# Both attention layers project a normed x with unsplit float32 weights, and the routing stage moves to VectorE

## The chip, the cores and the metric

One core of one Trainium2 chip runs the whole program. The metric is the device time of one execution in microseconds (us); three runs of the kernel before gave 1461.74, 1466.64 and 1473.64 us, the median is 1466.64 us.

## The reference

The input is 256 tokens of width 1024, in float32. Two transformer layers come first: layer 0 with the even mixer, layer 1 with the odd mixer, each with its MLP. A second block follows: a mixer with a context, then a mixture of 16 experts of which each token uses two.

```python
h = modulate(rms_norm(x, norm_mix[layer]), sh1, sc1)
u = h @ w_in                      # even: 1024 x 2976, odd: 1024 x 3072
...
q, k = rms_norm(q), rms_norm(k)   # per head, then rope, softmax(q k) v
x = x + g1 * (o @ w_out)
x = x + g2 * squared_relu_mlp(modulate(rms_norm(x), sh2, sc2))
...
scores = sigmoid(t @ w_router)    # moe: 16 experts in 4 groups of 4
g_idx = argmax(sum of the best two of each group)
out = out + gate[:, e:e + 1] * ((silu(a) * b) @ w_down[e])
```

The vectors sh1, sc1, g1, sh2, sc2, g2 are the columns of `silu(c) @ ada_w + ada_b`.

## The kernel before, in words

Tokens lie in two tiles of 128 (t = 0, 1). A product that needs full precision is made of three matmuls: weight and activation are each held as a rounded part "hi" (float32r) and the rest "lo", and `mm3` (L333 to L335) adds hi·hi, hi·lo and lo·hi in PSUM. A weight tile of 128 x 1024 is loaded into a "raw" tile by a DMA of SP's queue (L308), ACT casts it to hi (L321), and DVE subtracts to get lo (L322); in the even layer every fourth subtraction goes to POOL (`SHARE`). A raw tile is free again when lo is made. There are 4 raw, 5 hi and 5 lo tiles, and SP issues all loads in one order, so that a load that waits for its tile holds up the loads behind it.

- The even layer (`even`, phase 0). `first_columns` makes the normed x in columns and the first 672 projection columns (latents and rope key), with the scale and shift columns of layer 0 computed on the way by L755 from 8 MB of `adaN`. Then come two projections of 384 columns for the dilated values, the small projections `uq` and `ukv`, and four projections of 384 columns for dilated queries and keys, woven with the 8 heads of the first attention. `fill` puts 24 products of `adaT` (L458 on DVE, 512 KB each, two "ada" tiles) between them. The dilated attention and `even_out` follow.
- The first MLP (`mlp(0)`), 8 chunks, split weights.
- The odd layer (`odd`, phase 2). `norm_T` (called in the MLP's last chunk) leaves the normed x three times: hi in H0, lo in H1 and whole in A4. Query, key and value projections of the first attention (512 columns each) use `proj_steps` with hi and lo; the three of the second attention use `native_steps` (L378): one float32 matmul where `mm3` has three, with weights as they were loaded, into raw, hi and lo tiles in turn. A projection's epilogue `qk` runs over ACT (copy, square), POOL (rope halves L602, L603; reciprocal root L496, L497), DVE (L604, L605, L584, L636), then transposes on PE.
- The MLP of layer 1, the second block's mixer, then the routing: `before_route`, the `out2` projection with the router's logits behind each quarter, `route` (a chain of small DVE operations on 128 x 32 values), and `moe`, which normalises x into h2 on ACT, POOL and DVE (L1764 to L1773), splits it (L1777 on ACT, L1778 on POOL) and lets `experts` gather rows by one-hot matmuls (L1864) before the first expert product.

What differs between the two paths can be read from these lines:

```python
def split(self, hi, lo, src, scale=None, engine=None):      # L318
    ...
        self.nc.scalar.copy(hi, src)
        end = (engine or self.nc.vector).tensor_tensor(lo, src, hi, ALU.subtract)
...
def native_steps(self, st, hf, evac):                        # L371
    ws = sum([self.raw_unit(st) for _ in range(2)], [])
    ...
                    self.nc.tensor.matmul(pss[t], hf[:, k, t * P:t * P + P], ws[k], start=k == 0, stop=k == 7)
```

Of the kernel before, what the change touches and what calls it, by code (L numbers as in the profile page):

```python
# [11 lines left out]
F32R = mybir.dt.float32r  # L12
I32 = mybir.dt.int32
AF = mybir.ActivationFunctionType
ALU = mybir.AluOpType
# [25 lines left out]
EARLY_CONV = 1  # L41
ROPE_POOL = 1
# [3 lines left out]
SHARE = 4  # L46
# [6 lines left out]
EXTRA = [(), ("A4",), (), (), (), ()]  # L53
# [192 lines left out]
class Block:  # L246
# [114 lines left out]
    def raw_unit(self, st):  # L361

        ap, kt, w = st.next()
        ws = []
        for k0 in range(0, kt, 2):
            self.nnative += 1
            t = self.load(ap[:, k0 * w:k0 * w + 2 * w], ("raw", "hi", "lo")[self.nnative % 3])
            ws += [t[:, :w], t[:, w:2 * w]]
        return ws

    def native_steps(self, st, hf, evac):  # L371

        ws = sum([self.raw_unit(st) for _ in range(2)], [])
        pss = [self.ps(tag="pj") for _ in range(2)]
        for k0 in (0, 4):
            for t in range(2):
# [3 lines left out]
                if k0:  # L380
                    self.late.append([0, evac(t, pss[t], 512)])
                    yield
# [130 lines left out]
    def norm_T(self, rows, gates):  # L513
# [3 lines left out]
        hl = self.slot("H1", [P, 8, S], F32R)  # L517
        hh = self.slot("H0", [P, 8, S], F32R)
        self.h = hh, hl
        if self.phase == 1:  # L520
            self.hf = self.slot("A4", [P, 8, S])
        xns = self.slot("A0", [P, 2, D])
        for t, x in enumerate(self.x):
# [11 lines left out]
            for g in range(2):  # L535
# [7 lines left out]
                ends.append([nc.scalar.copy(hh[:, o, v], pv), V.tensor_tensor(hl[:, o, v], pv, hh[:, o, v], ALU.subtract)])  # L543
                if self.phase == 1:
                    nc.scalar.copy(self.hf[:, o, v], pv)
# [137 lines left out]
    def setup(self):  # L683
# [3 lines left out]
        c = self.T([P, CONST_W - 768], "consts")  # L687
# [33 lines left out]
        latents = self.first_columns()  # L721
        next(latents)
        nc.sync.dma_start(self.cols, A["cols"])
        self.trig(pf, inv)
        next(latents)
        nc.sync.dma_start(c[:, 178:434], A["consts"][:, 178:434])
        nc.sync.dma_start(c[:, 434:], A["consts"][:, 1202:])
        self.gains = self.slot("A5", [P, NGAIN1])
        nc.sync.dma_start(self.gains, A["gains"][:, :NGAIN1].to_broadcast([P, NGAIN1]))
        self.va = self.slot("A4", [P, 2048])  # L730
        nc.sync.dma_start(self.va[:, 1024:1792], A["consts"][:, 434:1202])
        self.dmasks = self.va[:, 1024:1792].rearrange("p (m k) -> p m k", m=3)
        self.gains2 = self.T([P, NGAIN - NGAIN1], "gains2")
        nc.sync.dma_start(self.gains2, A["gains"][:, NGAIN1:].to_broadcast([P, NGAIN - NGAIN1]))
# [33 lines left out]
    def first_columns(self):  # L768
# [16 lines left out]
        self.h = hh, hl = self.slot("H0", [P, 8, S], F32R), self.slot("H1", [P, 8, S], F32R)  # L785
# [3 lines left out]
        us = [self.unit(self.st) for _ in range(4)]  # L789
# [3 lines left out]
        us.append(self.unit(self.st))  # L793
        rooms = [self.slot(s, [P, 2, D]) for s in ("A4", "A5")]
        tiles.append([[r[:, i]] for r in rooms for i in range(2)])
        for t in tiles[2]:
            self.pe_load(t, 256)
        for (w, (c0, _)), ts in zip(PE_COLS, tiles):
            sums = self.ps(tag="po")
            for s, t in enumerate(ts):  # L800
                self.pe_part(sums, s, t, w)
# [5 lines left out]
            for k in range(j.start, j.stop):  # L807
                nc.scalar.activation(hh[:, k], xnT[:, k], AF.Identity, bias=cb[:, k:k + 1], scale=ca[:, k:k + 1])  # L808
                h = self.w(S)
                V.tensor_scalar(h, xnT[:, k], ca[:, k:k + 1], cb[:, k:k + 1], op0=ALU.mult, op1=ALU.add)  # L810
                V.tensor_tensor(hl[:, k], h, hh[:, k], ALU.subtract)
                wh, wl = us[k][:2]
                for i, (a, b) in enumerate(((0, 384), (384, 672))):
                    for t in range(2):
                        v = slice(t * P, t * P + P)
                        self.mm3(acc[i][t][:, :b - a], (hh[:, k, v], hl[:, k, v]), (wh[0][:, a:b], wl[0][:, a:b]), k == 0, k == 7)
                if len(us) < 8:
                    us.append(self.unit(self.st))
# [1267 lines left out]
```

## Time and profile before

| what | value |
|---|---|
| median of three runs | 1466.64 us |
| the profiled execution: its own time, its span | 1466.12 us, 1464.3 us |
| PE busy in the span | 1367.8 us (93%) |
| DVE, ACT, POOL busy | 1130.6, 834.2, 181.5 us |
| moved by DMA | 333.56 MB, 228 GB/s in the mean |

The shares are averages over stages with different limits, so the profile is read by stage: which engine is full in it, and which wait ends last. PE's busy time counts a matmul from its start to its modelled end, so that matmuls overlap; the pace of PE is the distance between starts. Stages of the program lie in the span so: first columns 0 to 46 us, the rest of the even layer to 222, its MLP to 405, the odd layer to 560, its MLP to 760, the mixer to 1120, routing to 1148, experts to the end.

### The profile page before, as it was taken

The page shows a single profiled execution, that of the slowest core. Times are in us where ns is not written, and L with a number is a line of the kernel's source. Part 1 is how long each engine was busy: PE and PEld are TensorE (multiplying, and loading weights), DVE is VectorE, ACT ScalarE, POOL GpSimd, SP SyncE. Part 2 cuts the span into 40 slices and gives each one's busy share as a digit, 9 for nine tenths or more (in the row PEclk, how much of TensorE's full clock was granted, in tenths as well). Part 3 has the DMA queues.
Part 4 walks back from the last instruction along what each step waited for, and adds up shares of the span by engine and source line. Part 5 has one row for each costly group of instructions (what it writes and reads, how often), then busy time and mean ns, then how long its engine had stood idle before and what let it go on. Part 6 is the DMA issues. An engine that isn't in the chain of part 4 may idle for free.

```text
span 1464.3 us, 20654 instructions
## 1 busy us (share of the span) xinstructions
PE 1367.8 (93%) x7402; PEld 1118.6 (76%) x7402; DVE 1130.6 (77%) x1880; ACT 834.2 (57%) x1329; POOL 181.5 (12%) x201
## 2 busy tenths in 40 slices
PE   6878889999999899999999999999996899999996
PEld 4767669888874467888989897677785788888884
DVE  4789867778784557799775789997766898888886
ACT  4565555445552464545764455655544687777774
POOL 0268420000053101000023000000003000000001
PEclk9989899999999989999999999999998899999998
DMA  9756547899944324878634766535552699999994
GB/s 350 251 181 226 172 144 248 305 326 322 333 146 147 113 87 139 285 269 300 233 105 137 241 234 205 173 124 169 177 180 87 214 359 338 330 328 322 319 346 147
DMA packets 93838, 333.56 MB, mean 228 GB/s; under 512 B 10656, under 2 KB 11808, under 8 KB 93216
## 3 DMA queue, kind: packets, MB, share of 16 engines
q1 hardware_dynamic: 93728, 332.17, 65.8%
q8 instruction: 60, 0.98, 0.3%
q14 instruction: 50, 0.41, 0.1%
HBM read 331.08 MB, written 1.05 MB: 227 GB/s over the span
## 4 chain that ended last, share of the span: by engine, by line
PE 62%; DVE 13%; DMA 11%; ACT 4%; issue 4%; POOL 4%; SPq 0%; POOLq 0%; ACTq 0%; DVEq 0%
PE pj L333 6%; PE pj L334 6%; PE pj L335 6%; PE ps L333 5%; PE ps L335 5%; PE ps L334 5%; DMA raw<-in_w_dram 5%; DMA ada<-in_adaT_dram 5%; PE ps L408 4%; DVE lo L322 3%; DVE ada L458 3%; PE pj L378 2%; ACT hi L321 2%; PE po L333 2%; PE po L335 2%
## 5 line engine op out<-in xcount | busy, mean ns | idle before, releaser
L321 ACT CAST hi<-raw 128x1024 fp32r<-128x1024 f32 (+3 forms) x325 | 327.3, 1018 | 230.8 <-DMA raw<-in_w_dram 70.5
L322 DVE TENSOR_TENSOR lo<-raw,hi 128x1024 fp32r<-128x1024 f32 (+4 forms) x315 | 380.3, 1218 | 99.4 <-ACT hi L321 96.8
L458 DVE CUSTOM_DVE_ANT_0 ada<-ada,crow 128x1024 f32<-128x1024 f32 x128 | 161.3, 1270 | 33.0 <-DMA ada<-in_adaT_dram 32.8
L333 PE MATMUL pj<-hi,H 128*128 128x512 f32 (+2 forms) x360 | 137.0, 384 | 5.7 <-ACT H L808 1.8
L334 PE MATMUL pj<-lo,H 128*128 128x512 f32 (+2 forms) x360 | 135.6, 378 | 5.1 <-DVE lo L322 4.3
L335 PE MATMUL pj<-hi,H 128*128 128x512 f32 (+2 forms) x360 | 133.3, 374 | 0.4 <-DVE H L543 0.4
L1191 PE MATMUL ps<-H,lo 128*128 128x256 f32 x408 | 116.0, 284 | 2.7 <-DVE lo L322 2.7
L333 PE MATMUL pj<-hi,A 128*128 128x512 f32 (+1 forms) x293 | 115.6, 395 | 2.1 <-DVE w L954 2.1
L334 PE MATMUL pj<-lo,A 128*128 128x512 f32 (+1 forms) x293 | 115.4, 394 | 1.1 <-DVE lo L322 0.9
L1189 PE MATMUL ps<-H,hi 128*128 128x256 f32 x408 | 116.0, 284 | 0.1
L1190 PE MATMUL ps<-H,hi 128*128 128x256 f32 x408 | 115.4, 283 | 0.0
L335 PE MATMUL pj<-hi,A 128*128 128x512 f32 (+1 forms) x293 | 114.4, 390 | 0.0
L333 PEld LDWEIGHTS pj<-hi,H 128*128 128x128 f32 x360 | 68.4, 191 | 22.4 <-issue 5.9
L334 PEld LDWEIGHTS pj<-lo,H 128*128 128x128 f32 x360 | 69.0, 192 | 17.0 <-DVE lo L322 7.0
L1191 PEld LDWEIGHTS ps<-H,lo 128*128 128x128 f32 x408 | 78.2, 192 | 3.9 <-DVE lo L322 3.9
L1189 PEld LDWEIGHTS ps<-H,hi 128*128 128x128 f32 x408 | 78.2, 192 | 0.9 <-ACT hi L321 0.3
L1190 PEld LDWEIGHTS ps<-H,hi 128*128 128x128 f32 x408 | 78.2, 192 | 0.4
L335 PEld LDWEIGHTS pj<-hi,H 128*128 128x128 f32 x360 | 68.3, 190 | 11.4 <-issue 1.9
L333 PE MATMUL ps<-hi,A 128*128 128x512 f32 x180 | 71.2, 396 | 0.0
L335 PE MATMUL ps<-hi,A 128*128 128x512 f32 x180 | 70.3, 391 | 0.0
L334 PE MATMUL ps<-lo,A 128*128 128x512 f32 x180 | 70.3, 390 | 0.0
L333 PEld LDWEIGHTS pj<-hi,A 128*128 128x128 f32 x293 | 55.5, 190 | 16.0 <-issue 4.4
(548 smaller groups left out, 3257.1 us busy)
## 6 DMA issues: line engine op xcount, KB each, us to landing
ada<-in_adaT_dram SPq DMA_DIRECT2D x128, 512.0 KB, 4.8
raw<-in_w_dram SPq DMA_DIRECT2D x128, 512.0 KB, 5.5
raw<-in_gu_dram SPq DMA_DIRECT2D x78, 512.0 KB, 5.9
raw<-in_in_dram SPq DMA_DIRECT2D x60, 512.0 KB, 4.5
raw<-in_down_dram SPq DMA_DIRECT2D x37, 512.0 KB, 5.6
crow<-in_gu_dram SPq DMA_DIRECT2D x34, 512.0 KB, 6.0
raw<-in_even_in_dram SPq DMA_DIRECT2D x24, 384.0 KB, 3.8
crow<-in_down_dram SPq DMA_DIRECT2D x18, 512.0 KB, 5.5
```

The costliest lines, as they stand in the source:

```text
L321: self.nc.scalar.copy(hi, src)
L322: end = (engine or self.nc.vector).tensor_tensor(lo, src, hi, ALU.subtract)
L333: mm(ps, ah, bh, start=start, stop=False)
L334: mm(ps, ah, bl, start=False, stop=False)
L335: mm(ps, al, bh, start=False, stop=stop)
L378: self.nc.tensor.matmul(pss[t], hf[:, k, t * P:t * P + P], ws[k], start=k == 0, stop=k == 7)
L408: self.nc.tensor.transpose(out, in_, self.ident[:p, :p])
L458: nc.vector.tensor_tensor_reduce(out=o, in0=wt, in1=r, scale=1.0, scalar=0.0, op0=ALU.mult, op1=ALU.add, accum_out=m[:, j:j + 1])
L1189: mm(ps[:, n % 2], wh, hh[:, k], start=k == 0 and n % 2 == 0, stop=False)
L1190: mm(ps[:, n % 2], wh, hl[:, k], start=False, stop=False)
L1191: mm(ps[:, n % 2], wl, hh[:, k], start=False, stop=k == 7 and n % 2 == 1)
```

## The change

- All six 384-column projections of the even layer, its first 672 columns, and the first three projections of the odd layer go through native float32 matmuls, one where there were three. No weight of `even_in` and `odd_in` is split; their tiles are used as loaded, from raw, hi and lo tiles in a fixed turn (`NATIVE`).
- The normed x of both layers is held once (`hf` in H0); hi and lo of it go, as do the cast and subtraction for them. In the odd layer the two halves are copied out of PSUM by ACT and DVE in turn.
- No subtraction goes to POOL in the even layer (`SHARE` goes); `uq`, `ukv` and `even_out` stay split, with DVE.
- In `first_columns` the gains are loaded earlier, masks and other constants later (behind the first value projection).
- Routing: the logits are made by float32 matmuls with tokens in rows from one unsplit x (`logits`); h2 starts as x·ar per quarter behind the residual sum, and becomes h2·rs + br by one DVE operation per token tile; hl is made by DVE behind the first one-hot mask; the first four expert tiles are loaded and split before the second half of `out2`; the first gather does all hi parts, then all lo parts, with DVE copying the latter.

```diff
-SHARE = 4
+NATIVE = ("raw", "hi", "lo") * 4 + ("hi", "lo")
-EXTRA = [(), ("A4",), (), (), (), ()]
+EXTRA = [(), ("A4",), ("A4",), (), (), ()]
...
         for k0 in range(0, kt, 2):
+            k1 = min(kt, k0 + 2)
             self.nnative += 1
-            t = self.load(ap[:, k0 * w:k0 * w + 2 * w], ("raw", "hi", "lo")[self.nnative % 3])
+            t = self.load(ap[:, k0 * w:k1 * w], NATIVE[self.nnative % len(NATIVE)])
...
-                ends.append([nc.scalar.copy(hh[:, o, v], pv), V.tensor_tensor(hl[:, o, v], pv, hh[:, o, v], ALU.subtract)])
-                if self.phase == 1:
-                    nc.scalar.copy(self.hf[:, o, v], pv)
+                if native:
+                    (V.tensor_copy if g else nc.scalar.copy)(self.hf[:, o, v], pv)
+                else:
+                    ends.append([nc.scalar.copy(hh[:, o, v], pv), V.tensor_tensor(hl[:, o, v], pv, hh[:, o, v], ALU.subtract)])
...
-        us = [self.unit(self.st) for _ in range(4)]
+        ws = [self.raw_unit(self.st)[0] for _ in range(4)]
...
+        def products(k):
+            for i, (a, b) in enumerate(((0, 384), (384, 672))):
+                for t in range(2):
+                    nc.tensor.matmul(acc[i][t][:, :b - a], hf[:, k, t * P:t * P + P], ws[k][:, a:b], start=k == 0, stop=k == 7)
+        columns(0)
+        for k in (0, 1, 2):
+            products(k)
+        columns(1)
+        products(3)
+        products(4)
+        columns(2)
+        for k in (5, 6, 7):
+            products(k)
...
-            self.proj(st, D, acts, f)
+            for _ in self.native_steps(st, self.hf, f):
+                pass
+            if c == 0:
+                nc.sync.dma_start(self.consts[:, 178:434], A["consts"][:, 178:434])
...
-                    yield from self.proj_steps(st, D, acts, f)
+                    yield from self.native_steps(st, self.hf, f)
...
-        for g in (qk_(("diff_q_norm", "diff_k_norm"), q1, False), val(v1, False)):
+        for g in (qk_(("diff_q_norm", "diff_k_norm"), q1), val(v1)):
...
-                self.out_T(self.x[t][:, j * 512:j * 512 + 512], self.xT, j * 4, t)
-                self.square(t, j)
+                self.to_T(o, self.x[t][:, s], 4, self.copied)
+                with self.behind(self.last_copy):
+                    self.square(t, j)
+                V.tensor_tensor(self.h2[:, t, s], self.x[t][:, s], self.ar[:, s], ALU.mult)
+                self.logits(t, range(4 * j, 4 * j + 4))
+            if j == 0:
+                self.sg = Stream(A["gu"], units(D, COLS_1024) * 16)
+                self.units0 = [self.expert_unit(self.sg) for _ in range(2)]
...
-        self.first = nc.scalar.copy(lT[:2 * NE], self.lps[:2 * NE, :S])
-        yield
-        for i in range(2):
-            nc.tensor.matmul(ps[:, i * NE:(i + 1) * NE], lT[:2 * NE, i * P:i * P + P], self.halves[:2 * NE], start=True, stop=True)
+        ps = self.lps
...
-        nc.scalar.mul(h2[:, 0], self.x[0], rs[0])
-        G_.tensor_tensor(h2[:, 0], h2[:, 0], self.ar, ALU.mult)
+        V.scalar_tensor_tensor(h2[:, 0], h2[:, 0], rs[0], self.br, op0=ALU.mult, op1=ALU.add)
...
-            G_.tensor_tensor(h2[:, 0], h2[:, 0], self.br, ALU.add)
-            V.scalar_tensor_tensor(h2[:, 1], self.x[1], rs[1], self.ar, op0=ALU.mult, op1=ALU.mult)
-        G_.tensor_tensor(h2[:, 1], h2[:, 1], self.br, ALU.add)
+        V.scalar_tensor_tensor(h2[:, 1], h2[:, 1], rs[1], self.br, op0=ALU.mult, op1=ALU.add)
...
-                G_.tensor_tensor(hl[:, t], h2[:, t], hh[:, t], ALU.subtract)
+                self.anchor[1:] = [V.tensor_tensor(hl[:, :, s], h2[:, :, s], hh[:, :, s], ALU.subtract)]
...
+            order = [(k2, q) for k2 in range(4) for q in range(2)] if g else [(k2, q) for q in range(2) for k2 in range(4)]
...
+                (V.tensor_copy if q and not g else nc.scalar.copy)(X[g][q][:, k2 * 2:k2 * 2 + 2], ps)
```

The scheduler sets each engine's order from this code. On PE at the start of the odd layer, where A is the normed x before its transposes (consts is the identity), H its transposed form and pj the projection's sum, the kernel before has:

```order
L408 MATMUL ps_3927<-consts_67,A_782_3902 128x128 x4
L333 MATMUL pj_4005<-hi_3983,H_780_3900 128x512
L334 MATMUL pj_4005<-lo_3984,H_780_3900 128x512
L335 MATMUL pj_4005<-hi_3983,H_779_3899 128x512
L333 MATMUL pj_4005<-hi_3983,H_780_3900 128x512
L334 MATMUL pj_4005<-lo_3984,H_780_3900 128x512
L335 MATMUL pj_4005<-hi_3983,H_779_3899 128x512
```

and the changed kernel has at the same place:

```order
L410 MATMUL ps_3515<-consts_67,A_708_3492 128x128 x4
L380 MATMUL pj_3571<-lo_3563,H_707_3491 128x512 x2
L380 MATMUL pj_3571<-raw_3565,H_707_3491 128x512
L410 MATMUL ps_3529<-consts_67,A_708_3492 128x128 x4
L410 MATMUL ps_3535<-consts_67,A_708_3492 128x128 x4
L380 MATMUL pj_3571<-raw_3565,H_707_3491 128x512
L380 MATMUL pj_3572<-lo_3563,H_707_3491 128x512 x2
```

Two rows of the weights take two matmuls in place of six, and the transposes of the second token tile stand behind three matmuls instead of behind twenty-two.

On DVE at the end of `out2`, where x, pj and w are residual, projection and product, A is h2 and es the routing's small tile, the kernel before has:

```order
L881 TENSOR_TENSOR w_10450<-pj_10389,row_10193 128x512
L882 TENSOR_TENSOR x_13_82<-x_13_82,w_10450 128x512
L504 SCALAR_TENSOR_TENSOR rs_10479<-ssx_79,rs_10479 128x1
L322 TENSOR_TENSOR H_2002_10256<-ps_10453,H_2001_10255 128x4x128
L1772 SCALAR_TENSOR_TENSOR A_2047_10476<-x_13_82,rs_10479,crow_10208 128x1024
L1716 SCALAR_TENSOR_TENSOR es_10491<-ps_10488,rs_10470,row_10241 128x16
L1716 SCALAR_TENSOR_TENSOR es_10491<-ps_10488,rs_10479,row_10241 128x16
L1718 TENSOR_SCALAR es_10491<-es_10491 128x32
```

and the changed kernel:

```order
L892 TENSOR_TENSOR x_13_82<-x_13_82,w_9908 128x512
L1780 SCALAR_TENSOR_TENSOR A_1900_9688<-A_1900_9688,rs_9924,crow_9657 128x1024
L1669 TENSOR_TENSOR A_1900_9688<-x_13_82,crow_9644 128x512
L1731 SCALAR_TENSOR_TENSOR es_9935<-ps_9763,rs_9924,row_9672 128x16
L506 SCALAR_TENSOR_TENSOR rs_9930<-ssx_79,rs_9930 128x1
L1731 SCALAR_TENSOR_TENSOR es_9935<-ps_9763,rs_9930,row_9672 128x16
L1783 SCALAR_TENSOR_TENSOR A_1900_9688<-A_1900_9688,rs_9930,crow_9657 128x1024
L1734 TENSOR_SCALAR es_9935<-es_9935 128x32
```

The wide operation of the second token tile has moved from ahead of the logits' first use to behind it, beside ACT's exponential; one wide and one half-wide operation stand ahead of it now, while x's transposes and squares are made.

## Rows read from the trace of the kernel before

**Rows 1.** The page's first part: busy time and share of the span, by engine.

```profile
PE 1367.8 (93%) x7402; PEld 1118.6 (76%) x7402; DVE 1130.6 (77%) x1880; ACT 834.2 (57%) x1329; POOL 181.5 (12%) x201
```

**Rows 2.** Stretches: us, busy PE, PEld, DVE, ACT, POOL, granted clock, DMA share, GB/s.

```profile
0.00:46.00 46.00, 32.12 (x232) 25.17 (x232) 21.91 (x91) 21.10 (x40) 2.11 (x10) 0.96 0.87 327
46.00:70.00 24.00, 20.73 (x108) 18.76 (x108) 19.21 (x35) 12.17 (x29) 10.25 (x15) 0.93 0.70 238
70.00:95.00 25.00, 18.83 (x88) 14.40 (x87) 18.04 (x40) 14.77 (x34) 18.28 (x29) 0.92 0.58 204
95.00:165.00 70.00, 60.22 (x319) 52.63 (x318) 63.51 (x130) 40.05 (x90) 54.36 (x47) 0.91 0.67 218
165.00:205.00 40.00, 38.68 (x222) 28.40 (x221) 31.12 (x82) 24.88 (x48) 4.35 (x3) 0.91 0.52 184
...
222.00:405.00 183.00, 177.75 (x1102) 159.92 (x1101) 142.92 (x187) 91.16 (x116) 0.73 (x2) 0.99 0.88 308
405.00:448.00 43.00, 38.71 (x178) 30.00 (x177) 34.27 (x59) 22.33 (x36) 22.65 (x20) 1.00 0.56 174
448.00:560.00 112.00, 105.42 (x402) 62.53 (x401) 60.93 (x176) 52.42 (x127) 16.98 (x22) 0.92 0.31 105
```

**Rows 3.** The chain of waits, 396 to 520 us: runs of native matmuls (start, us).

```profile
450.38 9.65 PE pj L378 x22
...
489.47 10.50 PE pj L378 x24
```

**Rows 4.** Timeline of PE: the even layer's projections, triples of 384 columns.

```profile
45.96 0.30 PE L335 MATMUL po<-hi,H 128*128 128x288 f32 x1
...
59.03 0.33 PE L333 MATMUL pj<-hi,H 128*128 128x384 f32 x1
...
59.55 0.33 PE L333 MATMUL pj<-hi,H 128*128 128x384 f32 x1
...
70.03 0.51 PE L333 MATMUL pj<-hi,A 128*128 128x384 f32 x2
```

**Rows 5.** Timeline of PE: a triple of 512 columns in the odd layer.

```profile
409.28 0.39 PE L333 MATMUL pj<-hi,H 128*128 128x512 f32 x1
...
409.96 0.39 PE L333 MATMUL pj<-hi,H 128*128 128x512 f32 x1
```

**Rows 6.** The subtractions of L322 alone, by stretch: DVE, POOL busy.

```profile
95.00:165.00 70.00, 19.51 (x17) 12.21 (x6) 0.91 0.67 218
```

**Rows 7.** The chain of waits from the odd layer's norm to its first scores.

```profile
410.46 1.14 DVE lo L322
...
442.70 0.61 DVE w L604
...
448.28 0.41 PE ps L665 x2
```

**Rows 8.** Timeline of DVE in the routing stage.

```profile
1119.95 0.68 DVE L881 TENSOR_TENSOR w<-pj,row 128x512 f32<-128x512 f32 x1
...
1124.27 3.36 DVE L1772 SCALAR_TENSOR_TENSOR A<-x,rs,crow 128x1024 f32<-128x1024 f32 x1
...
1128.22 1.88 DVE L1718 TENSOR_SCALAR es<-es 128x32 f32<-128x32 f32 x1 [0.30 <-ACT es L1717]
...
1130.52 1.89 DVE L1722 TENSOR_TENSOR es<-es,gains 128x32 f32<-128x32 f32 x1
1132.44 2.25 DVE L1726 TENSOR_TENSOR es<-es 128x24 f32<-128x24 f32 x1
1134.62 0.17 DVE L1727 TENSOR_TENSOR es<-es 128x16 f32<-128x16 f32 x1
```

**Rows 9.** Timeline of PE: the first one-hot gather and the first expert product.

```profile
1142.10 1.19 PE L1864 MATMUL po<-sc,O 128*128 128x256 f32 x4 [1.82 <-DVE row L1958]
...
1147.50 0.40 PE L333 MATMUL ps<-A,A 128*128 128x512 f32 x1
```

**Rows 10.** PE's waits in the expert stage, 1147 to 1445 us.

```profile
PE po L333 <- ACT A L1865: 0.4, 1, 0.4
```

More of the change, by code (lines that the diff above doesn't have):

```diff
@@ L792, in first_columns, with columns @@
             self.pe_load(t, 256)
-        us.append(self.unit(self.st))
-        rooms = [self.slot(s, [P, 2, D]) for s in ("A4", "A5")]
-        tiles.append([[r[:, i]] for r in rooms for i in range(2)])
+        ws += [self.raw_unit(self.st)[0] for _ in range(2)]
+        room = self.slot("A4", [P, 2, D])
+        tiles.append([[self.T([P, D], "crow", 2)] for _ in range(2)] + [[room[:, i]] for i in range(2)])
         for t in tiles[2]:
             self.pe_load(t, 256)
-        for (w, (c0, _)), ts in zip(PE_COLS, tiles):
+        ws += [self.raw_unit(self.st)[0] for _ in range(2)]
+        def columns(i):
+            w, (c0, _) = PE_COLS[i]
             sums = self.ps(tag="po")
-            for s, t in enumerate(ts):
+            for s, t in enumerate(tiles[i]):
                 self.pe_part(sums, s, t, w)
@@ L976, in kv_evac @@
             return f
-        self.share = SHARE
         for a, b in ((16, 24), (24, 40)):
@@ L1777, in moe, with low @@
                 nc.scalar.copy(hh[:, t], h2[:, t])
-                G_.tensor_tensor(hl[:, t], h2[:, t], hh[:, t], ALU.subtract)
+        M, sc, tmp = next(route)
+        def low():
+            for j in range(2):
+                s = slice(j * 512, j * 512 + 512)
+                self.anchor[1:] = [V.tensor_tensor(hl[:, :, s], h2[:, :, s], hh[:, :, s], ALU.subtract)]
+        self.low = low
         ps = self.ps()
@@ L1855, in gather @@
                 self.anchor[1:] = [last]
+                if self.low:
+                    with self.behind(last):
+                        self.low()
+                    self.low = None
             yield
             X[g] = [self.slot(f"A{g % 2 * 2 + q}", [P, 8, S], F32R) for q in range(2)]
[L1858 to L1866 removed]
+            order = [(k2, q) for k2 in range(4) for q in range(2)] if g else [(k2, q) for q in range(2) for k2 in range(4)]
+            for k2, q in order:
+                a = (hh, hl)[q]
+                ps = self.ps((P, 2, S), ("po", "ps")[q if g else k2 % 2])
+                for kk in range(2):
+                    k = k2 * 2 + kk
+                    for t in range(2):
+                        nc.tensor.matmul(ps[:, kk], a[:, t, k * P:k * P + P], pm[:, t].rearrange("p i s -> p (i s)"), start=t == 0, stop=t == 1)
+                (V.tensor_copy if q and not g else nc.scalar.copy)(X[g][q][:, k2 * 2:k2 * 2 + 2], ps)
+                yield
             for i in range(2):
```

121 lines of the change are left out of this document (50 added, 71 removed).

## The prediction

> **What bounds the kernel now.** The first thing to read is the page's line of busy time [rows 1]: PE is busy 1367.8 of 1464.3 us, DVE 1130.6, so almost every us that PE loses or saves should show in the time. That is an average. The second view, the windows by stage [rows 2], tells where it holds. In the first MLP (222 to 405 us) PE is busy 177.75 of 183 us and in the expert stage PE waits once, for 0.4 us, after its first product [rows 10]: both are bound by PE, and the change leaves their products alone. The stages that the change touches are limited otherwise. From 0 to 46 us PE looks full, but the DMA engines are at a share of 0.87 and 327 GB/s, the highest of the table. From 70 to 95 us POOL has 18.28 of 25 us and PE only 18.83. From 95 to 165 us DVE is the fullest, 63.51 of 70 us (91%), with PE at 60.22 and POOL at 54.36. From 165 to 205 us PE has 38.68 of 40. The odd layer's start (405 to 448 us) has PE at 38.71 of 43 us with a chain through DVE and POOL at its head and tail [rows 7]. The third view, the timeline, is for the routing: from DVE's last product sum at 1119.95 us [rows 8] to the first gather at 1142.10 us and the first expert product at 1147.50 us [rows 9] a chain of DVE operations decides, and PE has next to nothing.
>
> **The price of a native product.** The trace has native products already, in the second half of the odd layer: runs of 22 and 24 took 9.65 and 10.50 us [rows 3], together 20.15 us for 46, so 0.438 us for one of 512 columns. The three split matmuls for the same product start 0.68 us apart (409.28 to 409.96) [rows 5]. For 384 columns the split triple takes 0.52 us (59.03 to 59.55) [rows 4]. A native product of 384 isn't in the trace: by the share of columns 0.438 x 0.75 = 0.328 us, at most the 0.438 of the wider one, at least the 0.227 us of one split matmul of 512 (0.68 / 3) by the same share, 0.17. I take 0.328, the scaled row. For 288 columns likewise 0.39 split and 0.246 native. So a product saves 0.242 us at 512 columns, 0.192 at 384, 0.144 at 288. With 8 rows of weights and two token tiles, 16 products make a projection. PE saves 16 x (0.192 + 0.144) = 5.4 us in the first columns, 2 x 16 x 0.192 = 6.1 in the dilated values, 4 x 16 x 0.192 = 12.3 in dilated queries and keys, 3 x 16 x 0.242 = 11.6 in the odd layer: 35.4 us in all. How much of it is time depends on the stage.
>
> The Trainium skill speaks against this price: "FP8 and Floating Point Precision", section "TensorE Precision Notes", has true float32 take four passes through the array. Four passes at a third of the split triple would be 0.91 us for 512 columns; the rows show 0.438, about two passes, and the measurement decides. What four passes would make of the time is the last rival below.
>
> **Front and values, 0 to 70 us.** The next stage's first product, of `uq`, starts at 70.03 us [rows 4]; first columns end at about 46. PE's 5.4 + 6.1 us go, and with them ten subtractions and casts of weight tiles. What is late next is the DMA. What SP must bring up to the last value tile is, by the sizes in the code, x 1.05 MB, `adaN` 8.4, first columns 2.75, values 3.15, three fills of `adaT` 1.57, and the gains and constants that stand ahead, 1.9: 18.8 MB. At the 327 GB/s of the first 46 us that is 57.5 us, and PE is some 1.5 us behind the last tile. So `uq` starts at about 59 us, 11 us earlier. The rate held for 46 us so far, not for 58; I take -10. Bounds: -11.5 (all of PE's saving) and -3 (18.8 MB at the mean of the first 70 us, (327 x 46 + 238 x 24) / 70 = 296 GB/s, is 63.5 us, and 3 us more for the tail).
>
> **70 to 95 us.** `uq` and `ukv` stay split; the limit is the epilogue chain over POOL, which keeps its work. 0, with -6 as the end to which the free share of POOL (25 - 18.28) could shrink the stage.
>
> **95 to 165 us.** The four projections have 16 weight tiles. In this stretch DVE made 17 subtractions in 19.51 us (1.15 us each) and POOL 6 in 12.21 [rows 6]. Twelve on DVE go (-13.8 us), and `even_out`'s two from POOL's share come to DVE (+2.4). DVE then has 63.5 - 11.4 = 52 us, PE 60.2 - 12.3 = 48, POOL at most 42. With DVE at the same 91% the stage takes 57 us instead of 70: -13. The DMA allows it: up to 165 us the stages moved 327 x 46 + 238 x 24 + 204 x 25 + 218 x 70 = 41.1 MB, and at the first MLP's 308 GB/s that is 133 us, while the stage would now end at 165 - 10 - 13 = 142. That leaves little room, so I take -12. Bounds: 0, where the loads pace it at the old rate, and -16, PE's new 48 us at 89%.
>
> **165 to 205 us.** PE-bound; two subtractions wait on DVE (31.12 of 40 us) instead of POOL. 0, at worst +2.
>
> **Odd layer.** The first three projections take 48 x 0.438 = 21.0 us instead of 32.6, so PE's 38.71 us become 27. At the head DVE no longer makes lo of the normed x and of the first weights (the step at 410.46 us is one, 1.14 us [rows 7]) ahead of the second tile's norm, and the second tile's transposes stand behind three matmuls instead of 22. PE's idle time is 43 - 38.71 = 4.3 us; I count 2 of it as gained. At the tail the last key epilogue (DVE at 442.70, POOL, transposes, scores at 448.28, so 5.6 us, and some 2 us ahead of it) runs beside the value projection, which shrinks to 16 x 0.438 = 7.0 us; about 0.6 us of wait is new. -11.6 - 2 + 0.6 = -13. Bounds: -8 (the epilogues queue on POOL, 22.65 us of work in what would be 30) and -16 (all idle time goes). From 448 us on the products were native already: 0.
>
> **Routing.** On DVE the wide operation L1772, 3.36 us, stands in the chain; three small ones (L1718, L1722, L1726) take 1.88, 1.89 and 2.25 us while POOL runs the wide operations on h2, and their like takes 0.17 (L1727) when it doesn't [rows 8]. POOL's operations go, so these should fall to about 0.18 each: -5.5 us. In L1772's place stands L1783, not in the trace: at least the 0.68 us of a 512-wide operation, at most 3.36; two half-widths are 1.4, and it runs beside ACT's exponential. So -2 there. The lo part of h2 (two subtractions of 1.2 us by [rows 6]) stands on DVE behind the first mask, beside the hi gathers; if these don't hide it, +2.4. Logits in rows spare a copy and two transposes; counted at nothing. -7.5, bounds -3 and -10.
>
> **Experts.** PE waits for nothing; four tiles are there earlier: 0.
>
> **Sum.** -10 - 12 - 13 - 7.5 = -42.5 us. The profiled execution took 1466.12 us (span 1464.3 us), within 0.6 us of the median 1466.64, so no correction is needed: 1466.1 - 42.5 = 1423.6, say 1424 us. A measurement of this kernel can tell about 1%, 14.7 us, from no change.
>
> **Rivals.** (1) The even layer stays paced by its loads. For it: first columns and values come to the DMA's limit, and every product now waits for a tile directly, without a cast between that gave slack. Against: rates of 308 and 327 were held elsewhere. At the mean rate of the first 95 us, 272 GB/s, 41.1 MB take 151 us, not 142 to 143: +8.5, about 1432; at 258, the rate between this and the old mean of 249, 159 us: 1440.
> (2) The freed engines give more than counted: 70 to 95 us shrinks by 6, 95 to 165 and the odd layer by 16 each: 6 + 4 + 3 more, 1411. For it: POOL and DVE hinder each other in [rows 8], and POOL loses 12.21 us of subtractions in the crowded stage. Against: the 70 to 95 us stage is a chain of latencies.
> (3) The 22 us won in the even layer are given back in the first MLP, because its weights, at a DMA share of 0.88, come no earlier: 1424 + 22 = 1446. For it: 308 GB/s. Against: PE at 177.75 of 183 us there, so the loads keep ahead, and loads run ahead through free tiles as before.
> (4) Slower: native products cost more than the three that they replace, in the even layer's and odd layer's weights. Break-even is 0.68 us for 512 columns. At four passes of 0.227, 0.91 us, the odd layer gains 48 x 0.23 = 11 us, the even projections 96 x 0.173 = 17, the first columns 16 x 0.30 = 5; with routing's -7.5 this is +25, 1491 us. For it there is only the rule of four passes, from the Trainium skill's "FP8 and Floating Point Precision". Against it are the 46 products of [rows 3], which took less than half of that.
>
> **Chances.** Forecast 0.62, with a range of its own of 1412 to 1436; rival 1 0.18, rival 2 0.10, rival 3 0.07, rival 4 0.03. Rival 3's upper half, with part of rival 1's, reaches 1452 us, the bound of 1%: 0.03 of no change. So faster 0.94, same 0.03, slower 0.03. The range goes from 1406, below rival 2, to 1446, rival 3: it leaves out rival 4, half of rival 3 and the far end of rival 2, with what lies outside by a sum of unknown ends.
>
> **What would show it.** L380 at starts 0.44 us apart for 512 columns and 0.33 for 384; `uq`'s first product near 60 us (63 or later: rival 1); the stage of dilated queries and keys about 57 us long, its waits on DVE and not on DMA; the odd layer's norm to first scores 13 us shorter; the gap from the last product sum to the first expert product near 20 us instead of 27.6, with the small operations that follow L1718, L1722 and L1726 in the new code below 0.3 us each. The first MLP should be 183 us long still; 190 or more speaks for rival 3. L380 above 0.6 us for 512 columns would make the forecast wrong altogether.

## The result and the profile after

The changed kernel takes 1478.35 us in the median of 17 runs (1466.59 to 1482.03), the kernel before 1468.97 us beside it; the ratio is 1.0064 with a 95% interval of 1.0044 to 1.0083. The forecast was 1424 us, with a range of 1406 to 1446: a gain of 42 us was expected and a loss of 9 us came. The profiled execution of the changed kernel took 1482.03 us, its span is 1480.2 us: it is the slowest of the 17, so the two profiles stand 16 us apart where the medians stand 9 apart.

The page's line of busy time, to be held against [rows 1]:

```profile
PE 1394.9 (94%) x7238; PEld 1091.1 (74%) x7238; DVE 1079.8 (73%) x1838; ACT 793.0 (54%) x1268; POOL 132.5 (9%) x186
```

DVE lost 51 us of work, ACT 41, POOL 49, as the diff promises. PE gained 27 us where the prediction had taken 35 away. The windows of the changed kernel by stage, cut at the same events as [rows 2] (columns: stretch, length, busy PE, PEld, DVE, ACT, POOL, granted clock as a share of TensorE's full clock, DMA share, GB/s):

```profile
0.00:54.00 54.00, 38.35 (x200) 21.96 (x200) 12.12 (x72) 14.14 (x29) 2.79 (x11) 0.91 0.86 327
54.00:76.90 22.90, 21.92 (x75) 12.99 (x75) 13.40 (x32) 6.15 (x19) 3.35 (x11) 1.00 0.53 189
76.90:98.00 21.10, 16.61 (x79) 13.51 (x78) 14.90 (x35) 10.68 (x28) 14.49 (x24) 0.92 0.79 287
98.00:174.00 76.00, 64.86 (x256) 40.23 (x255) 52.50 (x134) 31.74 (x82) 36.76 (x45) 0.93 0.57 192
174.00:213.00 39.00, 38.92 (x230) 28.70 (x228) 26.22 (x71) 25.80 (x49) 0.44 (x1) 1.00 0.42 135
225.00:415.00 190.00, 184.05 (x1132) 163.35 (x1132) 144.18 (x188) 92.46 (x118) 0.73 (x2) 0.99 0.85 300
415.00:462.60 47.60, 45.75 (x131) 21.56 (x129) 19.82 (x46) 9.80 (x20) 17.74 (x20) 1.00 0.58 196
462.60:580.00 117.40, 110.57 (x408) 65.34 (x407) 65.09 (x182) 54.05 (x133) 19.17 (x25) 0.90 0.27 85
```

The reader is to see two things. The stage of dilated queries and keys (98 to 174 us) has 52.5 us of DVE, just what was forecast, and is 76 us long instead of the forecast 57, with PE at 64.86 where 48 were expected. The odd layer's start (415 to 462.6 us) has DVE at 19.82 of 47.6 us and PE at 45.75, at a full clock, where 27 were expected. The relief of DVE came; PE took it.

Why PE is fuller is seen in its timeline. First the even layer, native products of 384 columns, then the odd layer, of 512 (columns: start, us, engine, line, operation, tiles, sizes, count):

```profile
65.55 1.45 PE L380 MATMUL pj<-hi,H 128*128 128x384 f32 x4
66.84 1.45 PE L380 MATMUL pj<-lo,H 128*128 128x384 f32 x4
...
424.73 1.88 PE L380 MATMUL pj<-raw,H 128*128 128x512 f32 x4
426.45 1.88 PE L380 MATMUL pj<-hi,H 128*128 128x512 f32 x4
```

Four records of 384 columns start 1.29 us after the last four, so 0.32 us each, and of 512 columns 1.72 us, 0.43 each. These are the prices of the forecast (0.328 and 0.438). But a group of four records reads one weight tile for one half of the tokens, and a tile holds two rows of weights: that is two products, not four. All records of line L380 in the changed kernel, by the tile of the weights (count, shortest, median and longest in ns, first and last start in us, sizes):

```profile
L380 PE MATMUL pj<-hi,H x136: 483/591/1061, 56.1 to 509.5; 128*128 128x384 f32 x72, 128*128 128x512 f32 x64
L380 PE MATMUL pj<-lo,H x136: 483/592/1010, 61.7 to 517.1; 128*128 128x512 f32 x72, 128*128 128x384 f32 x64
L380 PE MATMUL pj<-raw,H x112: 483/540/1061, 54.6 to 518.9; 128*128 128x384 f32 x56, 128*128 128x512 f32 x56
```

That is 384 records. The program has 12 projections of 16 products, 192. The same count was there before the change, in the kernel before, for the three native projections that it had:

```profile
L378 PE MATMUL pj<-hi,A x32: 592/593/1061, 448.6 to 495.9; 128*128 128x512 f32 x32
L378 PE MATMUL pj<-lo,A x32: 592/593/1061, 451.3 to 503.6; 128*128 128x512 f32 x32
L378 PE MATMUL pj<-raw,A x32: 592/592/697, 456.4 to 505.3; 128*128 128x512 f32 x32
```

96 records for 48 products. The trace keeps two records for each native float32 product; [rows 3] counted records, and the prediction took them for products. So a product of 512 columns costs about 0.86 us, not 0.438, against 0.68 for the three split ones; of 384 columns 0.645 against 0.52.

The routing went as forecast. DVE's timeline from the last product sum on, which answers to [rows 8]:

```profile
1139.79 0.69 DVE L891 TENSOR_TENSOR w<-pj,row 128x512 f32<-128x512 f32 x1 [1.24 <-PE pj L335]
...
1145.48 1.27 DVE L1783 SCALAR_TENSOR_TENSOR A<-A,rs,crow 128x1024 f32<-128x1024 f32 x1
1146.68 0.17 DVE L1734 TENSOR_SCALAR es<-es 128x32 f32<-128x32 f32 x1
...
1147.27 0.19 DVE L1738 TENSOR_TENSOR es<-es,gains 128x32 f32<-128x32 f32 x1
1147.50 0.18 DVE L1742 TENSOR_TENSOR es<-es 128x24 f32<-128x24 f32 x1
```

and PE's, which answers to [rows 9]:

```profile
1155.08 1.20 PE L1885 MATMUL po<-sc,O 128*128 128x256 f32 x4 [1.82 <-DVE sc L1868]
...
1161.16 0.39 PE L333 MATMUL ps<-A,A 128*128 128x512 f32 x1
```

The three small operations fell from 1.88, 1.89 and 2.25 us to 0.17, 0.19 and 0.18, L1783 took 1.27 us where 1.4 was estimated, and the way from the last product sum to the first expert product is 21.4 us instead of 27.6.

### The profile page after: what moved, and what is told of

Its sections match the earlier page's. It is cut to its first block, busy times and chain, and to the rows that moved or that the text cites. A ratio compares the mean times of both kernels' runs of the same rounds, so it can differ in the third digit from the quotient of the medians.

```text
span 1480.2 us, 20182 instructions
## 1 busy us (share of the span) xinstructions
PE 1394.9 (94%) x7238; PEld 1091.1 (74%) x7238; DVE 1079.8 (73%) x1838; ACT 793.0 (54%) x1268; POOL 132.5 (9%) x186
## 5 line engine op out<-in xcount | busy, mean ns | idle before, releaser
L322 DVE TENSOR_TENSOR lo<-raw,hi 128x1024 fp32r<-128x1024 f32 (+2 forms) x279 | 337.1, 1218 | 106.4 <-ACT hi L321 104.5
L321 ACT CAST hi<-raw 128x1024 fp32r<-128x1024 f32 (+2 forms) x279 | 286.9, 1038 | 234.7 <-DMA raw<-in_w_dram 92.1
L460 DVE CUSTOM_DVE_ANT_0 ada<-ada,crow 128x1024 f32<-128x1024 f32 x128 | 156.2, 1228 | 42.2 <-DMA ada<-in_adaT_dram 42.0
L333 PE MATMUL pj<-hi,H 128*128 128x512 f32 (+1 forms) x192 | 76.1, 396 | 0.0
L334 PE MATMUL pj<-lo,H 128*128 128x512 f32 (+1 forms) x192 | 75.5, 393 | 0.0
L335 PE MATMUL pj<-hi,H 128*128 128x512 f32 (+1 forms) x192 | 74.3, 387 | 0.0
L333 PEld LDWEIGHTS pj<-hi,A 128*128 128x128 f32 x293 | 55.5, 190 | 18.2 <-issue 2.4
L322 DVE TENSOR_TENSOR lo<-crow,hi 128x1024 fp32r<-128x1024 f32 x52 | 62.5, 1222 | 7.2 <-ACT hi L321 6.7
L334 PEld LDWEIGHTS pj<-lo,A 128*128 128x128 f32 x293 | 55.5, 189 | 13.2 <-DVE lo L322 2.4
L335 PEld LDWEIGHTS pj<-hi,A 128*128 128x128 f32 x293 | 55.5, 189 | 10.8
```

What stands on the lines that cost most here:

```text
L333: mm(ps, ah, bh, start=start, stop=False)
L334: mm(ps, ah, bl, start=False, stop=False)
L335: mm(ps, al, bh, start=False, stop=stop)
L460: nc.vector.tensor_tensor_reduce(out=o, in0=wt, in1=r, scale=1.0, scalar=0.0, op0=ALU.mult, op1=ALU.add, accum_out=m[:, j:j + 1])
```

## The experiments

Two theories stood first: P, that a native product costs two records (0.86 us for 512 columns); and L, that it costs one and that loads take the gain. A third, S, came out of the first runs. Eleven kernels ran, each timed beside the kernel before. In the table a difference is that of the two medians (us) of the same comparison, the ratio has its 95% interval.

| run | median | difference | ratio |
|---|---|---|---|
| e1_route: new routing alone | 1461.28 | -9.4 | 0.994 (0.991 to 0.9971) |
| e2_odd: odd layer native alone | 1471.95 | +1.3 | 0.9986 (0.996 to 1.0011) |
| e3_even: even layer native alone | 1470.77 | +0.1 | 0.9997 (0.9973 to 1.0022) |
| e4_split: no native product in the odd layer | 1464.27 | -6.4 | 0.996 (0.9934 to 0.9987) |
| e5_half: changed kernel, narrow products | 1424.01 | -46.4 | 0.9706 (0.9662 to 0.9749) |
| e6_noroute: both layers native, old routing | 1480.99 | +10.6 | 1.0095 (1.0062 to 1.0128) |
| e7_route_split: e1 and e4 | 1457.38 | -13.1 | 0.9907 (0.9879 to 0.9935) |
| e8_twice: changed kernel, 48 products twice | 1517.47 | +47.0 | 1.0322 (1.0272 to 1.0371) |
| e9_rooms: changed kernel, other turn of tiles | 1471.06 | +0.8 | 1.0004 (0.9981 to 1.0026) |
| e10_before_rooms: before, other turn of tiles | 1464.34 | -6.0 | 0.9966 (0.994 to 0.9991) |
| e11_route_rooms: e1 and e10 | 1456.47 | -13.8 | 0.9884 (0.9855 to 0.9912) |

Where the profiles are compared below, the starts come from PE's timeline of each (us):

| start of | before | after | e5_half | e8_twice | e9_rooms | e10_before_rooms |
|---|---|---|---|---|---|---|
| first `uq` product | 70.03 | 76.86 | 65.67 | 76.27 | 74.55 | 70.97 |
| first scores, even layer | 98.61 | 102.41 | 92.18 | 102.99 | 100.56 | 99.58 |
| first dilated scores | 165.24 | 174.20 | 146.03 | 175.55 | 172.87 | 166.91 |
| first MLP, first product from a `hi` tile | 215.15 | 225.04 | 201.29 | 226.48 | 223.52 | 219.08 |
| odd layer's first product | 407.15 | 417.09 | 391.07 | 419.65 | 418.44 | 411.53 |
| odd layer's first scores | 448.21 | 462.63 | 423.06 | 506.39 | 463.99 | 452.58 |
| second MLP, first product of 256 columns | 577.20 | 594.29 | 534.17 | 636.82 | 585.72 | 575.11 |
| first gather | 1142.10 | 1155.08 | 1095.71 | 1197.79 | 1144.41 | 1138.77 |

In the text the two MLP rows are called the first and the second MLP for short. A single profile is good to a few us only: the first MLP starts at 215.15 us in the kernel before and at 219.08 in e10_before_rooms, with the same even layer.

**The parts alone.** e1_route is the kernel before with the new code from `out2` on:

```diff
-        nc.scalar.mul(h2[:, 0], self.x[0], rs[0])
-        G_.tensor_tensor(h2[:, 0], h2[:, 0], self.ar, ALU.mult)
+        V.scalar_tensor_tensor(h2[:, 0], h2[:, 0], rs[0], self.br, op0=ALU.mult, op1=ALU.add)
...
```

> The kernel before with the change of the routing stage alone. Both theories (the native products cost more than split ones; the native products are cheap and something else takes the gain back) leave this stage apart: the gap from the last product sum to the first expert product, 27.6 us before, should fall to about 21, and the time by 5 to 7.5 us. If it falls by less than 3 us, the routing is part of what went wrong.

It gained 9.4 us, more than the 5 to 7.5 expected here and inside the prediction's bounds of 3 to 10; in its profile the way from the last product sum to the first expert product is 20.2 us instead of 27.6. The routing isn't what went wrong.

e2_odd changes the first three projections of the odd layer, the norm's copies ahead of them, and the extra room A4:

```diff
-                yield from steps(f, native)
+                yield from self.native_steps(st, self.hf, f)
...
-EXTRA = [(), ("A4",), (), (), (), ()]
+EXTRA = [(), ("A4",), ("A4",), (), (), ()]
```

> The kernel before with the first three projections of the odd layer native, from one normed x; nothing else. Theory P (price): the trace keeps two records for each native product, so a product of 512 columns costs 2 x 0.43 = 0.86 us and not 0.438, against 0.68 for the split one; 48 products cost 48 x 0.18 = 8.6 us more, of which 2 to 4 come back at the stage's head: +4 to +7 us. Rival L (loads): the product is cheap, and waits for weight tiles take the gain: then PE shows waits for DMA in this stage, and without them the time would fall; -13 to 0 us.

The measured +1.3 us lies below theory P's range and just above L's; the interval by the ratio, -5.9 to +1.6, leaves P's range out. By the time alone, P missed. The stage itself speaks for P: from the odd layer's first product to its first scores the profile has 45.54 us, as in the changed kernel, where the kernel before has 41.06. Where the time came back is not shown.

e3_even changes the even layer alone:

```diff
-            self.proj(st, D, acts, f)
+            for _ in self.native_steps(st, self.hf, f):
+                pass
...
-                    yield from self.proj_steps(st, D, acts, f)
+                    yield from self.native_steps(st, self.hf, f)
```

> The kernel before with the even layer's change alone (native first columns, values, dilated queries and keys, order of the loads). Theory P: 96 products of 384 columns at 0.645 us instead of 0.52 cost 12 us, 16 rows of first columns some 3.6 us; what VectorE and GpSimd are relieved of gives back part of it where they were the bound (95 to 165 us): +4 to +12 us. Rival L: the products are cheap, PE waits for DMA in the front and the dilated stage; the time then lies between -22 and 0.

+0.1 us: below P's range again, and at the upper end of L's. The two layers alone cost nothing that can be measured, and together (e6_noroute, below) 10.6 us. That was the puzzle that led to theory S.

e4_split takes the native products out of the odd layer's second half instead:

```diff
-            yield from qk_(("moba_q_norm", "moba_k_norm"), q2, True)
-            yield from val(v2, True)
+            yield from qk_(("moba_q_norm", "moba_k_norm"), q2, False)
+            yield from val(v2, False)
```

> The kernel before with the odd layer's last three projections split as well, so that no native product is left in it. Theory P: 48 products go from 0.86 to 0.68 us on PE, -8.6 us if casts and subtractions keep up; -3 to -9 us. Rival L, with a native product at 0.438 us as the prediction had it: 48 x 0.24 = +11.6 us.

-6.4 us: theory L, by which it would have been 11.6 us slower, falls. It was taken for the price as well, too early, as e10_before_rooms shows.

**The price by itself.** e8_twice makes each native product of the odd layer's first three projections twice:

```diff
-                    self.nc.tensor.matmul(pss[t], hf[:, k, t * P:t * P + P], ws[k], start=k == 0, stop=k == 7)
+                    for i in range(self.twice):
+                        last = k == 7 and i == self.twice - 1
+                        self.nc.tensor.matmul(pss[t], hf[:, k, t * P:t * P + P], ws[k], start=k == 0 and i == 0, stop=last)
```

> The changed kernel with each native product of the odd layer's first three projections made twice (their sums are doubled), on a stretch where PE is full: the 48 more products are the price by itself. Theory P: 48 x 0.86 = +41 us, less what waits there now, so +36 to +42. Rival L, 0.438 us a product: +21 us or less.

The time rose from 1478.35 to 1517.47, 39 us for 48 products. The profile has it in the one stage: from the odd layer's first product to its first scores 86.74 us against 45.54, 41.2 us more, 0.858 us for a product. The page's line of busy time has 96 records more on PE for the 48 products (7334 against 7238), and PE's timeline shows eight records for four products, 3.43 us from start to start:

```profile
PE 1435.9 (94%) x7334; PEld 1108.8 (73%) x7334; DVE 1080.0 (71%) x1838; ACT 794.4 (52%) x1268; POOL 133.0 (9%) x186
```

```profile
425.57 3.60 PE L384 MATMUL pj<-raw,H 128*128 128x512 f32 x8
429.00 3.60 PE L384 MATMUL pj<-lo,H 128*128 128x512 f32 x8
```

This is theory P, shown.

**What the rest of the prediction was worth.** e5_half gives the products the price that the prediction had counted, by leaving out half of the columns in seven of eight:

```diff
-                    self.nc.tensor.matmul(pss[t], hf[:, k, t * P:t * P + P], ws[k], start=k == 0, stop=k == 7)
+                    n = w if k == 0 else w // 2
+                    self.nc.tensor.matmul(pss[t][:, :n], hf[:, k, t * P:t * P + P], ws[k][:, :n], start=k == 0, stop=k == 7)
```

> The changed kernel with seven of eight native products only half as wide (the right half of the columns of these products is left out of projections and first columns): with 0.86 us for a full product of 512 columns the mean is then 0.86 x (1 + 7 x 0.5) / 8 = 0.48 us, close to the 0.438 that the prediction counted. Theory P: with that price the rest of the prediction holds, some 35 to 45 us below the changed kernel in the first three projections of the odd layer and the even layer, and more where the odd layer's last three were native already: 1415 to 1445 us. Rival L (loads or chains take the gain): the loads are the same, the time stays within 10 us of the changed kernel.

1424.01 us, with products left out: loads and chains did not hold most of the gain back. That it meets the forecast to the digit is chance, since the sum is made otherwise. By the table of starts the odd layer begins 16.1 us earlier than in the kernel before (forecast for the even layer: 22), its first scores come 9.1 us sooner after that (forecast 13), and the way from there to the second MLP is 17.9 us shorter, in which the last three projections have their part: these were native before, and no forecast was made for them. The front is the exception: `uq` starts 4.4 us earlier than before, where 10 were forecast, so that at a low price too the front would have given less than half.

**Both layers, and neither.** e6_noroute is the whole change without its routing part; against the changed kernel:

```diff
-        V.scalar_tensor_tensor(h2[:, 0], h2[:, 0], rs[0], self.br, op0=ALU.mult, op1=ALU.add)
+        nc.scalar.mul(h2[:, 0], self.x[0], rs[0])
+        G_.tensor_tensor(h2[:, 0], h2[:, 0], self.ar, ALU.mult)
...
```

> The changed kernel with the routing stage of before: both attention layers native. The parts alone gave -9.4 us (routing), -2 (even +0, odd -2) against the kernel before, and all together +9.4. If the parts add up, as theory P has it with some 10 us more on PE, this is +10 to +18 us over before; if routing and layers hinder each other (a rival of its own: the early expert tiles or what follows on the loads), it is 0 to +3 us.

+10.6 us (by the ratio +9 to +19): the two layers together, inside theory P's range. It doesn't add up well with the rest, though: the changed kernel, which has the new routing besides, is at +9.4, so the medians give the routing 1 to 3 us here (by the differences or by 1480.99 - 1478.35) and 9.4 alone. In the profiles it shortens its stage here too, to 21.4 us from the 27.9 of e6_noroute. By the ratios it is worth 0.3%, give or take 0.4, which the 0.6% of e1_route doesn't contradict; whether layers and routing hinder each other stays open.

e7_route_split is e1_route with the edit of e4_split:

```diff
-            yield from val(v2, True)
+            yield from val(v2, False)
...
```

> The kernel before with the new routing stage and with the odd layer's last three projections split too: no native product at all. If the two add up (-9.4 and -6.4 us), 1453 to 1458 us, below both kernels. Rival L, with a native product cheaper than a split one, would have this above the run with the routing alone, 1461.

1457.38 us: the two gains add within 3 us, and this kernel is faster than both the kernel before and the changed one.

**The stall in the odd layer.** Together +10.6, alone +1.3 and +0.1: something in the single runs must have hidden the cost. For e3_even the profiles show what, a stall that the other kernels have on ACT, at the loads of the output projection. In the changed kernel, ACT's timeline:

```profile
486.07 1.03 ACT L321 CAST hi<-raw 128x1024 fp32r<-128x1024 f32 x1
492.89 1.04 ACT L321 CAST A<-raw 128x1024 fp32r<-128x1024 f32 x1 [5.78 <-DMA raw<-in_odd_out_dram]
...
494.79 0.49 ACT L650 COPY pt<-ps 128x384 f32<-128x384 f32 x1
```

and PE's beside it:

```profile
491.81 1.12 PE L380 MATMUL pj<-raw,H 128*128 128x512 f32 x2
495.34 1.65 PE L1289 MATMUL po<-A,pt 128*128 128x128 f32 x6 [2.41 <-ACT pt L650]
```

ACT stands for 5.78 us at a cast whose tile is not loaded; behind it in ACT's order are copies for which PE waits 2.41 us. SP's queue, from 440 to 540 us of the same profile and then of e9_rooms (below), tells why the tile is late:

```profile
SPq L308 <- PE pj L380: 34.5, 8, 13.9
```

```profile
SPq L308 <- PE pj L380: 27.7, 8, 6.9
```

Loads wait for tiles that native products still read (eight waits, 34.5 us in all, 13.9 the longest; in e9_rooms, which has no stall, the longest is 6.9). The kernel before has the same stall, PE waiting 4.12 us:

```profile
482.63 1.65 PE L1278 MATMUL po<-A,pt 128*128 128x128 f32 x6 [4.12 <-ACT pt L645]
```

Which rooms (the buffers of raw, hi and lo tiles) the last native weights use is set by a running count. In the kernels of before and after the last tile is a raw one. The native even layer alone moves the count, so that the last raw tile is the third from the end, and there is no such wait in that profile. In e2_odd the last tile is a hi one, and the one before it is raw; its wait is 2.02 us, so that the stall doesn't explain why e2_odd came out so cheap. e9_rooms, e10_before_rooms and e11_route_rooms have one line more, in the changed kernel, in the kernel before and in e1_route:

```diff
+        self.nnative += 2
         side = side()
```

> The changed kernel with the turn of weight tiles moved on by two ahead of the odd layer's last three projections, so that their last two tiles lie in hi and lo rooms and not the last one in a raw room. Theory S (stall): in the kernels of before and after, the first load of odd_out waits for a raw room that a native projection still holds, ScalarE's cast waits for the load, PE waits for copies queued behind the cast (4.1 us before, 2.4 us after, then a lower granted clock); the native even layer alone had moved this turn by chance, which hid its own cost. Without the stall -4 to -7 us against the changed kernel, 1471 to 1475. Rival: the turn does not matter, 1476 to 1480, and the even layer's cost comes from elsewhere.

> The kernel before with the same step of two in the turn. Theory S: the stall of 4.1 us and the lower clock behind it go, -4 to -7 us, about 1464, as much as splitting the last three projections gave (-6.4), which would mean that this gain came from the freed raw rooms rather than from the cheaper product. Rival: if the product's price made that gain, no change here, 1468 to 1472.

> The kernel before with the new routing and the step of two in the turn. Theory S: 1461.3 - 5 = 1455 to 1457 us, level with routing and all-split products (1457.4). Rival: 1461 us, as with the routing alone.

All three went as theory S has it: 1471.06 us against 1478.35 (-7.3), -6.0 us, and 1456.47 us. A window of 20 us from the same place, first of the changed kernel, then of e9_rooms (columns as above):

```profile
483.00:503.00 20.00, 17.59 (x51) 8.75 (x49) 12.71 (x35) 7.62 (x18) 6.10 (x7) 0.83 0.34 105
```

```profile
484.00:504.00 20.00, 20.00 (x63) 9.89 (x62) 15.71 (x48) 10.12 (x23) 7.33 (x9) 1.00 0.32 105
```

With the stall PE is idle for 2.4 us and its granted clock is 0.83 in the mean; without it 1.00. The two do not always go together, as e6_noroute shows, which has the changed kernel's turn and its wait:

```profile
493.39 0.94 PE L1289 MATMUL po<-A,pt 128*128 128x128 f32 x6 [2.42 <-ACT pt L650]
```

```profile
481.00:501.00 20.00, 17.58 (x57) 8.70 (x57) 12.98 (x35) 8.46 (x18) 7.46 (x8) 1.00 0.34 105
```

The profiles side by side, from the first odd scores to the second MLP:

| run | PE's wait behind the cast, us | length, us | granted clock |
|---|---|---|---|
| before | 4.12 | 128.99 | 0.93 |
| e1_route | 4.24 | 130.72 | 0.93 |
| e2_odd | 2.02 | 128.42 | 0.92 |
| after | 2.41 | 131.66 | 0.90 |
| e6_noroute | 2.42 | 124.35 | 0.96 |
| e3_even | none | 122.54 | 0.96 |
| e9_rooms | none | 121.73 | 0.96 |
| e10_before_rooms | none | 122.53 | 0.96 |
| e11_route_rooms | none | 127.16 | 0.91 |

The wait goes with the turn of the rooms in every run of the table. How much time follows it goes with the granted clock, which is low in e11_route_rooms without the wait and high in e6_noroute with it. So the 9.9 us between the changed kernel and e9_rooms in this table are not all the stall's, and its price is read from the medians: 7.3, 6.0 and, e11_route_rooms against e1_route, 4.8 us.

It follows also that freed raw tiles are enough for e4_split's gain (e10_before_rooms has -6.0 with the native products kept); that the cheaper product added anything there is not shown. Of the complete kernels e11_route_rooms and e7_route_split are the fastest; their intervals overlap.

## Why the prediction was wrong, point by point

**The failed step** is the price of a native product: "runs of 22 and 24 took 9.65 and 10.50 us [rows 3], together 20.15 us for 46, so 0.438 us for one of 512 columns". It was 0.438 us for one record, and a product has two. It measured 0.858 us (e8_twice). The step could have been caught in the trace of before: 96 records for three projections of 16 products each. Rival 4, to which 0.03 was given, is the mechanism that came: it set four passes of 0.227, 0.91 us. The Trainium skill had it so, in "FP8 and Floating Point Precision", section "TensorE Precision Notes" (true float32 takes four passes); the trace agrees, with 0.858 us, 3.8 times a third of the split triple. The prediction let its measurement decide against that page, and the measurement was misread. Rival 4's 1491 us were too many all the same: at the measured prices PE has 8.5 + 12.0 + 4.2 = 24.7 us more to do in both layers instead of 33, and not all of that became time, as the stages below show.

**The front** was forecast 10 us shorter with DMA as its bound. `uq` starts 6.83 us later. By the measured prices PE has 32 x 0.125 = 4.0 us more for the values, and a row of first columns takes about 2.35 us (the tile from 51.15 us on) against 2 x (0.52 + 0.39) = 1.82, so 4.2 for eight: 8.2 us. By place it is otherwise: the stage of first columns ends 8 us later (54 against 46) and the one of values is 1.1 us shorter (22.9 against 24.0). That loads bound the front is not borne out: in the first 54 us of the changed kernel PE's own waits for DMA come to 1.0 us. Nor was the price all that was wrong here, since e5_half had only 4.4 us of the 10; what held the rest was not followed.

**70 to 95 us**, counted at 0, became 3.0 us shorter from `uq` to first scores, inside the bounds given.

**95 to 165 us**, forecast -12: from first scores to dilated scores 71.79 us instead of 66.63, +5.2. DVE fell to 52.5 us as worked out. PE's 64 products of 384 columns cost 64 x 0.125 = 8.0 us more instead of 12.3 less, so PE is what is late; the relief gave back about 3.

**165 to 205 us and the first MLP** were counted at 0. From dilated scores to the first MLP's products it is 50.8 us instead of 49.9, and from there to the odd layer's first product 192.05, as before (192.00). Rival 3, a gain given back there, had no gain to take back here; e5_half, which had 13.9 us at the first MLP, kept them (189.8 us through it).

**The odd layer**, forecast -13: +4.5 us from its first product to its first scores. 48 x 0.178 = 8.5 us more on PE; 4 come back, of which 2.4 are idle time that the stage lost, about as forecast (PE idle 1.9 us of 47.6 instead of 4.3 of 43).

**Routing**, forecast -7.5: -6.2 us in the profiles of before and after, -9.4 in e1_route. Right in kind and size: the three small operations and L1783 in L1772's place come to -7.6. POOL's wide operations and the delays went together; no run moved POOL's alone.

**Experts**, counted at 0. They became some 2 us longer. The two windows, of the kernel before and then of the changed one, go from the first expert product to PE's last matmul (columns as above):

```profile
1147.50:1451.40 303.90, 303.06 (x1434) 251.12 (x1432) 265.48 (x270) 229.81 (x273) 0.00 (x0) 1.00 0.90 319
```

```profile
1161.16:1467.19 306.03, 305.04 (x1434) 251.00 (x1432) 266.71 (x273) 227.17 (x267) 0.00 (x0) 1.00 0.89 311
```

All six profiles with a native even layer have 306.0 to 307.1 us here and all seven with a split one 303.7 to 304.6, with the same 1434 records and a full clock. The routing is not the cause, as e3_even has it (306.85) and e1_route has not (303.72); why the same products run slower no run shows.

**The sum by the runs.** Routing gives -9.4 us (e1_route). Both layers cost 1471.06 - 1456.47 = 14.6 us, with the same routing and no stall in either (e9_rooms against e11_route_rooms). The stall costs 7.3 us after and 6.0 before, +1.3. Together +6.5, against the +9.4 measured. With the layers' cost from e6_noroute, 10.6 - 1.3 = 9.3 us, it would be +1.2. The medians are good to some 3 us each, so the layers' cost is known no better than 9 to 15 us. Of the 14.6 us the profiles place about 6.6 in the even layer (the first MLP starts at 224.6 us in the mean of five profiles with a native even layer, 218.0 in seven with a split one, which lie between 212.2 and 221.3), 3.9 in the odd layer's first half (45.5 against 41.6) and some 2 in the experts. The other 2 us lie within what single profiles differ by.

## What to carry to other kernels

Before a duration is made into a price, count the records of the line against the instructions that the program has: loops of 3 x 16 products with 96 records say that a record is half a product. A native float32 product spares the other engines a cast and a subtraction and costs PE about a quarter more than three split ones, so it can pay only where PE waits for those engines by more than that. Of the stages with native products only that of the values became shorter here, by 1.1 us. The one where DVE had been the fullest engine (63.51 us of 70, PE 60.22) became 5.2 us longer, since PE's extra work there was more than DVE's relief gave back. A weight tile that is used as loaded is held until its last product, so see which load comes next into that room and what stands in order behind its first use.

## What was not expected of the hardware

- A native float32 matmul leaves two records of 0.43 us for 512 columns, and 0.858 us in all; for 384 columns two of 0.32.
- One core moved about 400 GB/s over 20 us, 398 from 20 to 40 us in the changed kernel and 406 from 10 to 30 us in the kernel before; the 327 of [rows 2] is a mean over 46 us:

```profile
20.00:40.00 20.00, 18.17 (x91) 10.50 (x94) 3.29 (x25) 2.07 (x4) 0.00 (x0) 0.83 1.03 398
```

```profile
10.00:30.00 20.00, 17.92 (x102) 13.88 (x103) 8.32 (x22) 9.51 (x16) 0.00 (x0) 0.91 1.02 406
```

- After PE had stood idle for 2.41 us, up to 495.34 us, the granted clock of the changed kernel was 0.50, the lower of its two levels, from 496 to 500 us; in e6_noroute it stayed at 1.00 behind the same wait of 2.42 us. First the changed kernel, then e6_noroute:

```profile
496.00:500.00 4.00, 4.00 (x9) 2.13 (x9) 2.01 (x7) 1.41 (x5) 2.30 (x3) 0.50 0.50 139
```

```profile
494.00:498.00 4.00, 4.00 (x17) 2.13 (x16) 1.96 (x7) 2.39 (x8) 2.51 (x4) 1.00 0.68 200
```
